# Turning part of the activations by transposing transfers and reordering the end of the attention in a two-layer transformer trunk

## The chip, the cores and the metric

The kernel runs on one core of a Trainium2 chip. The metric is the device time of one execution in microseconds (us), the median of several runs. The engines of the core are named as in the profile: PE is TensorE's matmul pipe and PEld its weight load, DVE is VectorE, ACT is ScalarE, POOL is GpSimd and SP is SyncE, whose queue issues nearly all transfers here.

## The reference

A trunk of two layers works on 256 positions of width 1024. Each layer has a gated feed-forward block, a mixer of three attentions whose outputs are gated and summed, a second feed-forward block and a gated embedding term:

```python
for i in range(DEPTH):
    h = h + 0.5 * swiglu(rms_norm(h, norm_g[i, 0]), ffn1_wi[i], ffn1_wo[i])
    n = rms_norm(h, norm_g[i, 1])
    (aq, ak, av, bq, bkc, bvc, bks, bvs, bkw, bvw, bgate,
     cq, ck, cv, ga, gb, gc) = split_cols(n @ w_in[i], IN_SPLITS)
    ya = diff_attention(...)          # the first attention: aq, ak, av
    yb = nsa_attention(...)           # compressed, selected and windowed keys: b*
    yc = swa_sink_attention(...)      # sliding window with sinks: c*
    merged = (jax.nn.sigmoid(ga) * (ya @ w_branch[i, 0])
              + jax.nn.sigmoid(gb) * (yb @ w_branch[i, 1])
              + jax.nn.sigmoid(gc) * (yc @ w_branch[i, 2]))
    h = h + merged @ w_out[i]
    h = h + 0.5 * swiglu(rms_norm(h, norm_g[i, 2]), ffn2_wi[i], ffn2_wo[i])
    h = h + jax.nn.sigmoid(rms_norm(h, norm_g[i, 3]) @ w_ple_gate[i]) * (p[i] @ w_ple[i])
return rms_norm(h, final_norm)
```

All inputs are float32. The feed-forward width is 2816, each attention has a width of 512, and with 256 positions the selection of blocks in the second attention takes all of them.

## The kernel before

**Number format.** Every large product is done with each operand split into a high and a low part (`split`, line 225: ACT writes the high part, line 228, DVE the rest, line 223), and three matmuls high-high, high-low, low-high (`mul3`, lines 235 to 237). Weights arrive as one stream of tiles of 128x1024 (`load`, line 272): SP issues the transfer (line 278) into one of 4 `raw` buffers, `split` turns it into one of 6 `wh`/`wl` pairs. A product takes its tiles two or three ahead (`AHEAD`).

**Products.** `product` (line 305) runs over the k-tiles of 128 rows for the two position tiles t=0 and t=1. With the usual skew of 8 steps and 8 k-tiles it is first all of t=0, then all of t=1; one step of one tile is three matmuls. After the last k-tile of a position tile it calls `done`, which takes the result out of PSUM.

**Turning.** A matmul wants the left operand with the contraction on the partitions, so activations have to be transposed. `transposes` (line 239) does it on TensorE with the identity as the moving operand, 128x128 at a time, into a `tp` bank of PSUM (3 of them). `Norm.turn` (line 343) turns a half (c=0 or c=1) of a position tile of `h` so, 4 transposes into the bank `nt`, and then ACT and DVE split it with the norm's gain into `nT` (lines 336 and 340). In the attention, `toT` (line 518) turns queries and keys into the bank `qt`: for the first attention from `done_a`, for the second from `done_q` (`qB`) and `done_bk` (`kB`, its second half of columns), for the third from `done_q` (`qC`) and `done_ck` (`kC`, two blocks).

**Turning by transfers.** The feed-forward's gated activations go another way already, `turn_by_dma` (line 436): DVE cuts the float32 values into their two 16-bit halves (`cut`, line 442), SP issues two transposing transfers (`flip`, line 443), and one f-group later `collect` has DVE put the halves together again (`whole`, line 448).

**Attention.** The projections run in the order A0, A1, A2, Ck, Cq, Bk, Bv, Bq. The three attentions are generators in lanes of `Flow` (line 156): each k-step of a product calls `tick`, which advances a lane by a fraction of a step (PACE_A, PACE_B, PACE_C), so that their small pieces lie between the large matmuls. The first attention's branch follows (`branch`, line 954: a gate product, then the branch product `br`), then the compression of the second attention's keys (`compress`, whose rest `compressed` runs in a lane of its own), the branch of the third attention, and last the branch of the second. In this last branch both gate products run first, then `flow.join` finishes the second attention, then the `br` products run for both tiles, column half by column half; `mix` (line 964) adds them to `merged`, turns that on TensorE (`mt`) and splits it to `mT`, which the product `wo` needs.

**The second attention's end.** `attend_b` (line 839) works on units of (group g, position tile t). The last part of a unit multiplies the compressed scores `pcT[t]`; these come from `attend_cmp` (line 803): 12 small matmuls `sc`, a chain of small DVE and ACT operations on `pc` (lines 811 to 822), one transpose `pct` and a copy. It is called inside the unit that first needs them, so that for t=1 it comes near the end.

**Who sets the order.** The program is written in one order, and a scheduler at build time fixes the order of each engine's instructions from it, by readiness and by place in the program; `done` has a higher priority. At run time each engine goes through its list in order and waits at semaphores.

Of the kernel before, what the change touches and what calls it, by code (L numbers as in the profile page):

```python
# [33 lines left out]
PACE_A, PACE_B, PACE_C = 0.75, 0.75, 0.6  # L34
# [121 lines left out]
class Flow:  # L156
# [22 lines left out]
    def join(self, side):  # L179
        while any(s is side for lane in self.lanes.values() for s, _ in lane[0]):  # L180
            for lane in self.lanes.values():
                if lane[0]:
                    self.step(lane)
# [3 lines left out]
def trunk(ctx: ExitStack, tc: tile.TileContext, a: dict, out: bass.AP, index: list):  # L187
    nc = tc.nc
# [20 lines left out]
    def tp_bank(name):  # L209
        return bank("tp", 3, name)  # L210
# [93 lines left out]

    def product(lhs, nk, done, name, w, skew=SKEW):

        def run():
            ps = [None] * NT
            for step in range(nk + skew):
                for t, k in ((0, step), (1, step - skew)):  # L310
# [10 lines left out]
        return run  # L321


    class Norm:
# [18 lines left out]
        def turn(self, t, c):  # L343
            ps = tp_bank("nt")
# [87 lines left out]
    def halves(x):  # L432

        return x.bitcast(U16).rearrange("p (n w) -> p n w", w=2)

    def turn_by_dma(pool, src, m):


        cut = stage("cut").bitcast(U16).rearrange("p (w n) -> p w n", w=2)
        flip = pool.tile([128, 2, 4, 128], U16, tag="flip", bufs=3, name="flip")  # L440
        for w in range(2):
            nc.vector.tensor_copy(cut[:, w, :128 * m], halves(src)[:, :128 * m, w])
            nc.sync.dma_start(flip[:, w, :m], cut[:, w, :128 * m], transpose=True)

        def collect():
            whole = stage("whole")
            for w in range(2):
                tc.keep_in_program_order(nc.vector.tensor_copy(  # L448
                    halves(whole)[:, :128 * m, w], flip[:, w, :m].rearrange("p a b -> p (a b)")))
            return whole[:, :128 * m].rearrange("p (k q) -> p k q", q=128)  # L450
        return collect

    def ffn(i, n, norm, after, aside=None):
# [14 lines left out]
        def gated(f):  # L468
            def done(t, ps):
# [6 lines left out]
                if f % 2 or f == FG - 1:  # L476
                    first, m = f - f % 2, 2 * (f % 2 + 1)
                    pending[t] = 2 * first, m, turn_by_dma(pool, held[t], m)
# [25 lines left out]
    def attention(i, norm, after):  # L504
# [10 lines left out]
        def heads(name):  # L515
            return blk(name).rearrange("p x (k t) q -> p x k (t q)", k=4)

# [137 lines left out]
        def done_bk(t, ps):  # L655
# [3 lines left out]
            for c in range(2):  # L659
# [13 lines left out]
                else:  # L673
                    toT(kB[0], t, slice(0, 4), srcs)
# [15 lines left out]
        def done_q(dst, name):  # L690
            def done(t, ps):
# [4 lines left out]
                toT(dst[0], t, slice(0, 4), [sb[:, 128 * k:128 * k + 128] for k in range(4)])  # L696
# [13 lines left out]
        def compress():  # L710
# [22 lines left out]
            c_sb[0] = pool.tile([128, 512], F32, name="c_sb")  # L733
            nc.vector.tensor_copy(c_sb[0][:64], c_ps[:64])

        def compressed():
# [46 lines left out]
            kc[0] = kt  # L783

# [447 lines left out]
```

## Time and profile before

| | us |
|---|---|
| median of 3 runs | 1357.85 |
| lowest and highest of the 3 | 1355.42, 1359.24 |
| the profiled execution | 1356.52 |
| its span from the first to the last instruction | 1354.7 |
| PE busy in the span | 1331.4 |
| DVE busy | 947.4 |
| ACT busy | 782.2 |

The times of instructions below are from the profiled execution. PE's busy time counts matmuls that overlap: a matmul of 512 columns lasts 390 ns in the record, but the next one starts 227 ns after it. What PE's work costs is therefore read from the distance between starts, not from durations. Layer 2 repeats layer 1 some 668 us later. In layer 1 the mixer runs from about 191 us to 475 us.

### The profile page before, as it was taken

Reading aid. Unit: us, or ns where it says so; the run is one execution under the profiler, and the core shown is the slowest. Engines: PE = TensorE matmul, PEld = TensorE weight load, DVE = VectorE, ACT = ScalarE, POOL = GpSimd, SP = SyncE. Lnnn points to the kernel's source line nnn. Section 1 sums busy time; section 2 is a strip of 40 time slices with the busy share of each in tenths; the row PEclk is TensorE's granted clock in tenths of the full one; section 3 lists DMA queues with packets and bytes.
Section 4 is the critical chain, followed back from the end, with each engine's and each line's share of the span. In section 5 each row is a group of like instructions: output and inputs, shape, how many; then the busy total and the mean of one; then the engine's idle time right before and its main releaser. Section 6 shows DMA issues by size and latency. Waiting matters only on the chain.

```text
span 1354.7 us, 18246 instructions
## 1 busy us (share of the span) xinstructions
PE 1331.4 (98%) x6414; PEld 1096.5 (81%) x6414; DVE 947.4 (70%) x1795; ACT 782.2 (58%) x1382; POOL 18.5 (1%) x36
## 2 busy tenths in 40 slices
PE   9999999999998999999999999999999989999997
PEld 7778888887886788888888888888788868888886
DVE  7677566768887767665767765577697776767565
ACT  7555455668655655544755544566795645545454
POOL 0000000000000000000000000000000000000000
PEclk9999999999999999999999999999999989999999
DMA  8797665444642577775567765645456425887662
GB/s 306 205 275 224 194 226 169 152 166 155 231 154 64 185 201 220 206 221 180 189 198 216 229 202 193 227 151 177 162 186 205 140 65 184 220 222 210 194 204 84
DMA packets 121993, 257.14 MB, mean 190 GB/s; under 512 B 56944, under 2 KB 62500, under 8 KB 121902
## 3 DMA queue, kind: packets, MB, share of 16 engines
q1 hardware_dynamic: 121150, 254.34, 60.5%
q0 software_dynamic: 320, 1.08, 0.3%
q8 instruction: 50, 0.82, 0.2%
q10 hardware_dynamic: 432, 0.56, 0.1%
q14 instruction: 41, 0.34, 0.1%
HBM read 243.33 MB, written 1.08 MB: 180 GB/s over the span
## 4 chain that ended last, share of the span: by engine, by line
PE 92%; DVE 3%; DMA 2%; ACT 2%; issue 1%; SPq 0%; POOLq 0%; POOL 0%; DVEq 0%; ACTq 0%
PE ff L236 11%; PE ff L237 11%; PE ff L235 11%; PE fo L236 6%; PE fo L235 6%; PE fo L237 6%; PE gate L235 3%; PE gate L237 3%; PE gate L236 3%; PE s L537 3%; PE A L236 2%; PE A L235 2%; PE A L237 2%; PE br L236 1%; PE br L235 1%; PE br L237 1%
## 5 line engine op out<-in xcount | busy, mean ns | idle before, releaser
L223 DVE TENSOR_TENSOR wl<-raw,wh 128x1024 fp32r<-128x1024 f32 (+1 forms) x448 | 539.8, 1213 | 176.5 <-ACT wh L228 169.3
L228 ACT ACTIVATE wh<-raw 128x1024 fp32r<-128x1024 f32 (+1 forms) x448 | 467.6, 1050 | 231.6 <-PE fo L237 84.9
L236 PE MATMUL ff<-wl,nT 128*128 128x512 f32 x704 | 273.6, 390 | 2.0 <-DVE wl L223 1.9
L237 PE MATMUL ff<-wh,nT 128*128 128x512 f32 x704 | 273.4, 390 | 0.0
L235 PE MATMUL ff<-wh,nT 128*128 128x512 f32 x704 | 270.8, 391 | 0.0
L236 PEld LDWEIGHTS ff<-wl,nT 128*128 128x128 f32 x704 | 132.2, 188 | 31.3 <-DVE wl L223 4.0
L235 PEld LDWEIGHTS ff<-wh,nT 128*128 128x128 f32 x704 | 132.4, 188 | 29.3 <-ACT wh L228 0.8
L237 PEld LDWEIGHTS ff<-wh,nT 128*128 128x128 f32 x704 | 132.3, 188 | 27.1
L236 PE MATMUL fo<-wl,gT 128*128 128x512 f32 x352 | 134.2, 392 | 0.0
L237 PE MATMUL fo<-wh,gT 128*128 128x512 f32 x352 | 133.7, 389 | 0.0
L235 PE MATMUL fo<-wh,gT 128*128 128x512 f32 x352 | 132.5, 389 | 0.0
L474 ACT ACTIVATE act<-ff,stats 128x256 f32<-128x256 f32 x88 | 41.4, 472 | 86.0 <-PE ff L237 85.8
L475 DVE TENSOR_TENSOR gated<-act,ff 128x256 f32<-128x256 f32 x88 | 36.6, 417 | 65.0 <-ACT act L474 65.0
L235 PEld LDWEIGHTS fo<-wh,gT 128*128 128x128 f32 x352 | 66.1, 188 | 13.9
L235 PE MATMUL gate<-wh,nT 128*128 128x512 f32 x192 | 77.0, 403 | 0.0
L237 PEld LDWEIGHTS fo<-wh,gT 128*128 128x128 f32 x352 | 66.1, 188 | 13.3
L236 PEld LDWEIGHTS fo<-wl,gT 128*128 128x128 f32 x352 | 66.1, 188 | 13.3
L236 PE MATMUL gate<-wl,nT 128*128 128x512 f32 x192 | 75.9, 395 | 0.0
L237 PE MATMUL gate<-wh,nT 128*128 128x512 f32 x192 | 75.8, 395 | 0.0
L228 ACT ACTIVATE gT<-whole 128x512 fp32r<-128x512 f32 (+1 forms) x48 | 28.4, 591 | 62.8 <-DVE whole L448 62.6
L548 ACT ACTIVATE p<-p,st 128x128 f32<-128x128 f32 (+1 forms) x128 | 56.7, 445 | 11.4 <-DVE st L546 11.0
L448 DVE COPY whole<-flip 128x512 uint16<-128x512 uint16 (+1 forms) x96 | 38.2, 434 | 12.8 <-DMA flip<-cut 12.2
(301 smaller groups left out, 2003.2 us busy)
## 6 DMA issues: line engine op xcount, KB each, us to landing
raw<-in_wst SPq DMA_DIRECT2D x438, 512.0 KB, 4.4
band<-table SPq DMA_DIRECT2D x10, 512.0 KB, 4.9
raw<-in_wbv SPq DMA_DIRECT2D x4, 420.0 KB, 3.2
flip<-cut SPq DMA_TRANSPOSE x96, 4.0
xt<-in_xt SPq DMA_DIRECT2D x4, 256.0 KB, 5.2
raw<-in_wst SPq DMA_DIRECT2D x4, 256.0 KB, 3.5
h<-in_x SPq DMA_DIRECT2D x2, 512.0 KB, 7.9
band<-table POOLq DMA_DIRECT2D x2, 512.0 KB, 6.7
```

Source lines behind the costliest of these rows:

```text
L223: nc.vector.tensor_tensor(o, x, y, op=ALU.subtract)
L228: nc.scalar.activation(hi, src, AF.Copy)
L235: nc.tensor.matmul(ps, xh, wh, start=start, stop=False)
L236: nc.tensor.matmul(ps, xh, wl, start=False, stop=False)
L237: nc.tensor.matmul(ps, xl, wh, start=False, stop=stop)
L448: tc.keep_in_program_order(nc.vector.tensor_copy(halves(whole)[:, :128 * m, w], flip[:, w, :m].rearrange("p a b -> p (a b)")))
L474: nc.scalar.activation(act, ps[:, :256], AF.Silu, scale=norm.r(t))
L475: nc.vector.tensor_tensor(held[t][:, 256 * (f % 2):256 * (f % 2) + 256], act, ps[:, 256:], op=ALU.mult)
L537: nc.tensor.matmul(o, q[r, x, qb[m], t * 128:(t + 1) * 128], kk, start=x + y == 0, stop=x == 1)
L548: nc.scalar.activation(p[j], p[j], AF.Exp, bias=st[:, j:j + 1], scale=-1.0, accum_out=st[:, n + j:n + j + 1])
```

## The change

Four things are edited. **First**, `turn_by_dma` is moved out so that all stages can use it, with `flip` in the pool `base` and 2 buffers where it had 3 in the feed-forward's pool, and `Norm.turn` uses it for the half c=0 of each position tile; the half c=1 stays on TensorE. **Second**, `toT_late` does the same for `kB`, `qB`, `qC` and `kC` in the attention. Both put off the second part (`whole` and the split) by 12 product steps, with `later` and `on_time`. **Third**, `attend_cmp` for both position tiles moves to the end of `compressed`, the lane that prepares the compressed keys, and the unit of the second attention only waits until `pcT[t]` is there; PACE_B goes from 0.75 to 0.72. **Fourth**, in the last branch the `br` products are ordered by position tile: t=0 for both column halves as soon as both groups of t=0 are done (`readyB[0] == 2`), then the join, then t=1. To make room, `c_sb` takes a buffer of the tag `th`.

```diff
--- before.py
+++ after.py
@@ -31,7 +31,7 @@
 AHEAD = 2
 RAWS = 4
 WBUFS = 6
-PACE_A, PACE_B, PACE_C = 0.75, 0.75, 0.6
+PACE_A, PACE_B, PACE_C = 0.75, 0.72, 0.6
 
 
 
@@ -176,8 +176,8 @@
                     lane[1] -= 1.0
                     self.step(lane)
 
-    def join(self, side):
-        while any(s is side for lane in self.lanes.values() for s, _ in lane[0]):
+    def join(self, side, ready=lambda: False):
+        while not ready() and any(s is side for lane in self.lanes.values() for s, _ in lane[0]):
             for lane in self.lanes.values():
                 if lane[0]:
                     self.step(lane)
@@ -302,11 +302,24 @@
                 done(t, ps, s)
         return run
 
+    deferred = []
+
+    def later(steps, act):
+
+        deferred.append([steps, act])
+
+    def on_time():
+        for d in deferred:
+            d[0] -= 1
+        while deferred and deferred[0][0] <= 0:
+            deferred.pop(0)[1]()
+
     def product(lhs, nk, done, name, w, skew=SKEW):
 
         def run():
             ps = [None] * NT
             for step in range(nk + skew):
+                on_time()
                 for t, k in ((0, step), (1, step - skew)):
                     if 0 <= k < nk:
                         wh, wl = w(k)
@@ -320,6 +333,27 @@
                         flow.tick()
         return run
 
+    def halves(x):
+
+        return x.bitcast(U16).rearrange("p (n w) -> p n w", w=2)
+
+    def turn_by_dma(src, m):
+
+
+        cut = stage("cut").bitcast(U16).rearrange("p (w n) -> p w n", w=2)
+        flip = base.tile([128, 2, 4, 128], U16, tag="flip", bufs=2, name="flip")
+        for w in range(2):
+            nc.vector.tensor_copy(cut[:, w, :128 * m], halves(src)[:, :128 * m, w])
+            nc.sync.dma_start(flip[:, w, :m], cut[:, w, :128 * m], transpose=True)
+
+        def collect():
+            whole = stage("whole")
+            for w in range(2):
+                tc.keep_in_program_order(nc.vector.tensor_copy(
+                    halves(whole)[:, :128 * m, w], flip[:, w, :m].rearrange("p a b -> p (a b)")))
+            return whole[:, :128 * m].rearrange("p (k q) -> p k q", q=128)
+        return collect
+
 
     class Norm:
         def __init__(self, row):
@@ -341,6 +375,10 @@
                                                T[:, 0, k + m, :].bitcast(F32), op0=ALU.mult, op1=ALU.subtract)
 
         def turn(self, t, c):
+            if c == 0:
+                whole = turn_by_dma(h[:, t, :512], 4)
+                later(12, lambda: self.turned(t, 0, whole().rearrange("p k q -> p (k q)")))
+                return
             ps = tp_bank("nt")
             transposes(ps, [h[:, t, 512 * c + 128 * k:512 * c + 128 * k + 128] for k in range(4)])
             self.turned(t, 4 * c, ps)
@@ -429,27 +467,6 @@
...
-    def turn_by_dma(pool, src, m):
...
-        flip = pool.tile([128, 2, 4, 128], U16, tag="flip", bufs=3, name="flip")
...
@@ -475,7 +492,7 @@
                 nc.vector.tensor_tensor(held[t][:, 256 * (f % 2):256 * (f % 2) + 256], act, ps[:, 256:], op=ALU.mult)
                 if f % 2 or f == FG - 1:
                     first, m = f - f % 2, 2 * (f % 2 + 1)
-                    pending[t] = 2 * first, m, turn_by_dma(pool, held[t], m)
+                    pending[t] = 2 * first, m, turn_by_dma(held[t], m)
             return done
 
         def gathered(t, k):
@@ -514,6 +531,12 @@
 
         def heads(name):
             return blk(name).rearrange("p x (k t) q -> p x k (t q)", k=4)
+
+        def toT_late(dst, t, n, src):
+
+            whole = turn_by_dma(src, n)
+            ts = slice(t * 128, (t + 1) * 128)
+            later(12, lambda: split(dst[:, 0, :n, ts], dst[:, 1, :n, ts], whole()))
 
         def toT(dst, t, blocks, srcs):
 
@@ -671,7 +694,7 @@
                         r = slice(64 * par, 64 * par + 64)
                         nc.vector.tensor_copy(half[0][r, :, t * 64:(t + 1) * 64], v[r, :, :, par])
                 else:
-                    toT(kB[0], t, slice(0, 4), srcs)
+                    toT_late(kB[0], t, 4, sb)
 
         def values(v, ps, scale):
 
@@ -693,7 +716,7 @@
                     dst[0] = heads(name)
                 sb = stage()
                 nc.scalar.activation(sb, ps, AF.Copy, scale=norm.eighth(t))
-                toT(dst[0], t, slice(0, 4), [sb[:, 128 * k:128 * k + 128] for k in range(4)])
+                toT_late(dst[0], t, 4, sb)
             return done
 
         w1 = w2 = None
@@ -730,7 +753,7 @@
                     nc.tensor.matmul(o, both, wh, start=k == 0, stop=False)
                     nc.tensor.matmul(o, both, wl, start=False, stop=k == 15)
                     flow.tick()
-            c_sb[0] = pool.tile([128, 512], F32, name="c_sb")
+            c_sb[0] = pool.tile([128, 512], F32, tag="th", bufs=4, name="c_sb")
             nc.vector.tensor_copy(c_sb[0][:64], c_ps[:64])
 
         def compressed():
@@ -781,6 +804,9 @@
             vc[0] = pool.tile([128, 1, 128], F32R, name="vc")
             values(vc[0], v_ps[:, :64], None)
             kc[0] = kt
+            yield
+            for t in range(NT):
+                yield from attend_cmp(t)
 
         def weighted(y_ps, v, T, start, stop):
 
@@ -798,7 +824,7 @@
             v = tmp.rearrange("p (m q) -> p m q", m=2)
             split(y[:, 0, 2 * g:2 * g + 2, :], y[:, 1, 2 * g:2 * g + 2, :], v)
 
-        yB, pcT = [None] * NT, {}
+        yB, pcT, readyB = [None] * NT, {}, [0] * NT
 
         def attend_cmp(t):
             s_ps = tp_bank("sc")
@@ -883,14 +909,13 @@
                         weighted(y_ps[g, t], vB[0][:, x, k, g], T.rearrange("p x j q -> p x (j q)"), x == 0 and k == 0, False)
                         yield
                 if ss[-1] == 1:
-                    if t not in pcT:
-                        while kc[0] is None:
-                            yield
-                        yield from attend_cmp(t)
+                    while t not in pcT:
+                        yield
                     T = own(t, g)
                     yield
                     weighted(y_ps[g, t], vc[0][:, 0], T.rearrange("p x j q -> p x (j q)"), False, True)
                     gather(yB[t], y_ps[g, t], g)
+                    readyB[t] += 1
                     yield
 
             yield from pipelined([(g, t, ss) for t, sets in ((0, [(0, 1)]), (1, [(0,), (1,)])) for g in range(2) for ss in sets], first, second)
@@ -907,7 +932,7 @@
             dst = sb[:, :256].rearrange("p (x u d) -> p x u d", u=2, d=64)
             nc.scalar.activation(dst[:, :, 0, :], src, AF.Copy, scale=norm.r(t))
             nc.vector.tensor_scalar(dst[:, :, 1, :], src, norm.r(t), None, op0=ALU.mult)
-            toT(kC[0], t, slice(0, 2), [sb[:, 0:128], sb[:, 128:256]])
+            toT_late(kC[0], t, 2, sb)
             values(vC[0][:, t], ps[:, 128:256], norm.r(t))
 
         def attend_c():
@@ -987,9 +1012,22 @@
             if last:
                 for c in range(2):
                     yield gated(c, both[c][0])
+                ws = [streamed(i, f"br{b}{c}", 512) for c in range(2)]
+
+                def tile(t):
+                    for c in range(2):
+                        ps = product_bank(f"br{t}")
+                        for k in range(4):
+                            wh, wl = ws[c](k)
+                            mul3(ps, yT[t][:, 0, k, :], yT[t][:, 1, k, :], wh, wl, k == 0, k == 3)
+                            flow.tick()
+                        with tc.high_priority(offset=150):
+                            both[c][1](t, ps)
+
+                yield lambda: flow.join(sides[side], lambda: readyB[0] == 2)
+                yield lambda: tile(0)
                 yield lambda: flow.join(sides[side])
-                for c in range(2):
-                    yield mixed(c, both[c][1])
+                yield lambda: tile(1)
             else:
                 for c in range(2):
                     yield gated(c, both[c][0])
```

## Rows read from the trace of the kernel before

**Rows 1.** The page's first part: busy time, share, instructions of each engine.
```profile
PE 1331.4 (98%) x6414; PEld 1096.5 (81%) x6414; DVE 947.4 (70%) x1795; ACT 782.2 (58%) x1382; POOL 18.5 (1%) x36
```
**Rows 2.** PE's waits, whole span: who waited for whom; us, times, longest.
```profile
PE pct L243 <- DVE pc L822: 6.2, 2, 3.3
PE pt L243 <- DVE pT L223: 1.9, 2, 0.9
PE mt L243 <- DVE merged L969: 1.3, 2, 0.6
```
**Rows 3.** Stretches: length, busy PE, PEld, DVE, ACT, POOL, clock, DMA share, GB/s.
```profile
220.00:300.00 80.00, 80.00 (x471) 68.02 (x470) 54.95 (x133) 52.20 (x121) 2.78 (x4) 1.00 0.47 156
300.00:360.00 60.00, 60.00 (x344) 48.37 (x343) 54.91 (x147) 52.82 (x127) 0.00 (x0) 1.00 0.59 194
...
409.63:446.66 37.03, 30.92 (x153) 23.62 (x151) 29.97 (x62) 21.98 (x44) 0.00 (x0) 1.00 0.27 85
1077.63:1115.78 38.15, 32.60 (x153) 25.89 (x151) 30.18 (x62) 22.00 (x44) 0.00 (x0) 0.91 0.27 83
1092.80:1099.20 6.40, 5.10 (x22) 4.78 (x23) 4.77 (x10) 3.01 (x7) 0.00 (x0) 0.50 0.00 0
```
**Rows 4.** PE's groups by shape: count, then busy us and mean ns.
```profile
L243 PE MATMUL nt<-ident,h 128*128 128x128 f32 x112 | 16.8, 272 | 0.0
...
L243 PE MATMUL qt<-ident,stage 128*128 128x128 f32 x88 | 15.0, 275 | 0.0
```
**Rows 5.** PE in order of time around one `nt` group: start, us, instruction.
```profile
159.47 0.39 PE L237 MATMUL fo<-wh,gT 128*128 128x512 f32 x1
159.70 0.39 PE L235 MATMUL fo<-wh,gT 128*128 128x512 f32 x1
159.93 0.60 PE L243 MATMUL nt<-ident,h 128*128 128x128 f32 x4
160.29 0.48 PE L236 MATMUL fo<-wl,gT 128*128 128x512 f32 x1
160.60 0.40 PE L237 MATMUL fo<-wh,gT 128*128 128x512 f32 x1
```
**Rows 6.** PE in order of time around the two transposes of `kC`.
```profile
234.85 0.28 PE L236 MATMUL Ck<-wl,nT 128*128 128x256 f32 x1
234.97 0.38 PE L243 MATMUL qt<-ident,stage 128*128 128x128 f32 x2
235.10 0.37 PE L237 MATMUL Ck<-wh,nT 128*128 128x256 f32 x1
```
**Rows 7.** DVE's groups by shape: the copies of turning by transfers.
```profile
L448 DVE COPY whole<-flip 128x512 uint16<-128x512 uint16 x80 | 34.1, 459 | 12.8 <-DMA flip<-cut 12.2
L442 DVE COPY cut<-gated 128x512 uint16<-128x512 uint16 x80 | 30.5, 423 | 1.3
...
L448 DVE COPY whole<-flip 128x256 uint16<-128x256 uint16 x16 | 4.1, 307 | 0.0
L442 DVE COPY cut<-gated 128x256 uint16<-128x256 uint16 x16 | 3.9, 288 | 0.1
```
**Rows 8.** The tile `flip`: issue min/median/max in ns, then time to landing.
```profile
L443 SPq DMA_TRANSPOSE flip<-cut x96: 1179/1210/2118, 31.4 to 1261.6; - x96
...
DMA to landing us min/median/max: 2.3/4.0/7.4
```
**Rows 9.** DVE's and SP's waits, whole span: us in total, times, longest.
```profile
DVE whole L448 <- DMA flip<-cut: 12.2, 15, 1.9
SPq L278 <- DVE wl L223: 524.7, 229, 24.7
```
**Rows 10.** DVE, then PE, at the second attention's end in layer 1.
```profile
419.42 0.28 DVE L811 TENSOR_TENSOR pc<-sc,cbias 128x128 f32<-128x128 f32 x1
...
425.22 0.29 DVE L822 TENSOR_TENSOR pc<-pc,cmask 128x128 f32<-128x128 f32 x1
...
425.57 0.33 PE L243 MATMUL pct<-ident,pc 128*128 128x128 f32 x1 [2.81 <-DVE pc L822]
```

More of the change, by code (lines that the diff above doesn't have):

```diff
@@ L429, in finished @@
             queue.dma_start(out[t * 128:(t + 1) * 128, 512 * k:512 * k + 512], y[k])
-    def halves(x):
-        return x.bitcast(U16).rearrange("p (n w) -> p n w", w=2)
-    def turn_by_dma(pool, src, m):
-        cut = stage("cut").bitcast(U16).rearrange("p (w n) -> p w n", w=2)
-        flip = pool.tile([128, 2, 4, 128], U16, tag="flip", bufs=3, name="flip")
[L441 to L451, printed above, removed]
     def ffn(i, n, norm, after, aside=None):
```

## The prediction

> **What bounds the kernel now.** I read the page's busy times first, then the table of stretches, then PE's waits. PE is busy for 1331.4 of 1354.7 us, DVE for 70% [rows 1]. The stretches show where that share is honest: from 220 to 360 us, where all queries and keys are turned, PE is busy without a break [rows 3], and the waits list names no other place of size than the end of the second attention [rows 2]. Busy PE there means matmuls started back to back: starts of 512 columns stand 0.23 us apart [rows 5]. So outside the attention's end each instruction taken from PE's list shortens the span by its place in the row of starts, as long as weights keep coming. The attention's end is the exception: 37.03 us with 30.92 busy in layer 1, 38.15 with 32.60 in layer 2 [rows 3]. The 6.1 and 5.6 us of idle PE are mostly one wait, the transpose `pct` behind DVE's chain on `pc` (2.8 and 3.3 us) [rows 2, 10]. In layer 2 PE, after that wait, shows a granted clock of 0.50 for 6.4 us [rows 3], the 1.2 GHz level, where layer 1 stays at 2.4 GHz; the same work from gate to `wo` takes 38.15 - 37.03 = 1.1 us longer.
>
> **Transposes taken from PE.** All `nt` transposes are 112 [rows 4], 28 groups of 4; half of them, the 14 groups of c=0, go. Of the 88 `qt` transposes [rows 4] the first attention keeps 32; 12 groups of 4 (`kB`, `qB`, `qC`: two position tiles, two layers) and 4 groups of 2 (`kC`) go. What a group costs is the distance between starts, not 4 x 272 ns: 159.93 to 160.29 is 0.36 us, and the next matmul is followed after 0.31 instead of 0.23, another 0.08 [rows 5]. Two transposes of `kC` take 0.13 [rows 6]. Lower bound: 26 x 0.36 + 4 x 0.13 = 9.9 us; upper, with 0.08 for each group, 12.2 us. The 0.08 is paid where large matmuls follow, as at `nt`; queries and keys often stand beside other small matmuls. I take 14 x 0.44 + 12 x 0.36 + 4 x 0.13 = **11.0 us**, all on the path.
>
> **The end of the second attention.** Moving `attend_cmp` to its own lane takes the chain on `pc` out of the end; there it lasted from 419.42 to 425.51, most of it in DVE's queue behind other pieces [rows 10]. Its 12 `sc` matmuls and one transpose per position tile run earlier, inside products, at the same price. The new `br` order lets 24 matmuls of t=0 (24 x 0.23 = 5.5 us) and the first `wo` matmuls of t=0 run while the last unit of t=1 is finished. At stake are 6.1 + 5.6 us of idle and 1.1 us of clock, 12.8 us; the floor is 0, if the idle only changes its name. What comes last next: weights. The `br` tiles of both halves stay until t=1 is through and take 4 of the 6 `wh`/`wl` pairs, so that only two `wo` tiles are ready; the others are split in the same microseconds in which DVE mixes t=1. Today's waits for `merged` (0.6 us a layer) [rows 2] are of this kind. I leave 1.6 us a layer and take 12.8 - 3.2 = **9.6 us**. The pace of 0.72 only spreads fewer steps; I cost it at nothing, covered by the gate products beside which they lie.
>
> **What it adds.** A moved group of 4 costs DVE two cuts and two copies back, 2 x 0.423 + 2 x 0.459 = 1.76 us, a group of 2 costs 2 x 0.288 + 2 x 0.307 = 1.19 [rows 7]. Over the span that is 26 x 1.76 + 4 x 1.19 = 51 us more, DVE at about 75%: not the bound as a mean. ACT and DVE split as before, from SBUF instead of PSUM; that price I put at nothing, bounded by the 20 to 30 ns by which like groups differ. By stretches it is tighter. From 220 to 360 DVE is busy 54.95 + 54.91 of 140 us, with 5.1 us free in the last 60 [rows 3]. Each layer adds 6 x 1.76 + 2 x 1.19 = 13 us here, which fits into the 30 us free as a sum, but `qB` falls at the edge of the full part. There is no row for DVE falling behind here. Its cost lies between 0 and the two late groups of `qB` with their 3.5 us a layer, 7 us in all; I take **1.5 us**, nearer to 0 because weights are split ahead. Below 0 is excluded: DVE only gains work.
>
> SP issues 60 more transposing transfers at 1.21 us each [rows 8], 73 us of its queue. What is behind one is the weight stream: the issue waits for its `cut`, and the next `raw` transfer with it. SP now waits 525 us for DVE to free a `raw` buffer [rows 9], so it runs ahead; I cost this at nothing, and without that cover it would be one transfer's 2.4 us pair per group, in the tight part only. The DMA share there is 0.47 to 0.59 [rows 3] and leaves room. DVE waits for a landing at the head of `whole`, with the weight splits behind it. From `done` to the second landing: 0.42 + 1.21 + 4.0 = 5.6 us; 12 steps of three matmuls give 12 x 0.68 = 8.2 us. Behind `Ck` and inside `Bv`, with narrow matmuls, they give about 5 us, so two groups a layer may wait for around 1 us. In the feed-forward 96 such copies cost DVE 12.2 us of waits [rows 9]. `flip` with 2 buffers instead of 3 holds at most one turn of each position tile: nothing.
>
> The Trainium skill, page "VectorE: DVE Perf Modes", section "Rules for kernel authors", speaks against the change: a 128x128 transpose belongs on TensorE if PSUM will do as its destination, and the section "The three transpose paths" gives 390 ns there against 1309 ns by transfer (bf16). Charged at 390 ns a piece, the 112 removed transposes would be an estimated 43.7 us, four times what the starts in the rows say; charged at 1309 ns for each half, the transfers would look far dearer, yet they are on no engine that is full.
>
> **Sum.** 1356.5 - 11.0 - 9.6 + 1.5 = **1337 us**, from the profiled execution (span 1354.7, 1.8 around it). It is 1.3 below the median of the runs shown; that is inside the range below and not added.
>
> **Rivals.** (1) *The end of the attention is only moved.* The wait for `pct` goes, but PE then waits for `wo` weights or `mT` as long. For it: the buffers above, and a DMA share of 0.27 there [rows 3], a stream that stands still. Against: 24 ready matmuls where there were 12. Time: 1356.5 - 11.0 + 1.5 = 1347.
>
> (2) *DVE becomes the bound from 220 to 360, and the kernel is slower than before.* The mechanism: `whole` stands at the head of DVE's list until its transfer has landed, and the weight splits wait behind it. Of the 30.1 us that DVE has free there, 13.0 go to copies and 2.4 to a shorter stretch, 14.7 are left. Eight groups a layer with a mean wait w stall PE by 8w - 14.7. The gain of 20.6 us, 10.3 a layer, is eaten at w = 25.0 / 8 = 3.1 us. For it: with the longest landing, 7.4 us [rows 8], a group needs 9.0 us against 8.2, or 4 us more than it has inside `Bv`. Against: the median is 4.0 and the longest wait seen 1.9 [rows 8, 9]; all eight would have to be late. At w = 3.5 the stall is 13.3 a layer: 1356.5 - 20.6 + 26.6 = 1363. The rule of the Trainium skill's page "VectorE: DVE Perf Modes", section "Rules for kernel authors", would show itself here: a slower path whose delay is too short.
>
> (3) *Everything lands.* Upper price of the transposes, no idle left, DVE free: 1356.5 - 12.2 - 12.8 = 1331.5.
>
> (4) *It doesn't do what it says.* The transposes go, but PE's list waits for `nT`, `qB` or weights in their place, and the end of the attention keeps its length: 1355.
>
> **How the numbers follow.** Forecast 1337 (its own range 1332 to 1343): 0.55. Rival 1: 0.17. Rival 2: 0.09. Rival 3: 0.12. Rival 4: 0.07. The measurement tells about 0.3% (4 us) from no change. Faster: 0.55 + 0.17 + 0.12 = 0.84; same: rival 4, 0.07; slower: 0.09. The range reaches from below rival 3, by the 1.1 us between the profiled execution and the fastest run and some rounding, to above rival 1: 1329 to 1350. It leaves out rivals 2 and 4 and little else.
>
> **What would show it.** `nt` falls to 56 and `qt` to 32, `flip` rises from 96 to 156 issues; the wait of `pct` is gone from PE's waits, and the stretch from the last gates to `wo` loses 4 to 6 us a layer with the clock at 1.00 in both. Where t=0's half c=0 ends in `fo`, the starts stay 0.23 us apart instead of 0.36 across the `nt` group. Right on DVE: its busy time is near 998 us, its wait for `flip` stays under 30 us, and PE stays unbroken from 220 to 360. Wrong: PE waits for `wl` in 300 to 360, or for `whole` through `nT` or `qB`, or a new wait of 3 us or more between the `br` and `wo` products.

## The result: slower by 0.5%

The changed kernel takes 1364.76 us (median of 4 runs, 1363.40 to 1366.04), the kernel before 1357.55 beside it: ratio 1.0054, interval 1.0036 to 1.0072. The forecast was 1337 us, with a range of 1329 to 1350. The profiled execution took 1364.21 us, its span 1362.4 against 1354.7.

The page's first part of the changed kernel answers to [rows 1]. PE has 112 instructions less, as forecast, and DVE 38 us more work, where 51 were forecast; but PE's busy time fell by 5.3 us only, and 7.7 us were added to the span.

```profile
PE 1326.1 (97%) x6302; PEld 1089.0 (80%) x6302; DVE 985.5 (72%) x1915; ACT 780.8 (57%) x1382; POOL 19.7 (1%) x36
```

PE's waits in the changed kernel (us in total, times, longest) answer to [rows 2]. `pct` is gone. New is a wait of 5.5 us in each layer, `ct` behind `stage<-Bk` on DVE, and there are smaller ones at the end of the attention and ahead of the feed-forwards. `ct` is the transpose of `Bk`'s result for the compression; `stage<-Bk` is the instruction that takes this result out of PSUM, its evacuation.

```profile
PE ct L243 <- DVE stage L687: 11.0, 2, 5.5
PE mt L243 <- DVE merged L994: 3.4, 2, 1.7
PE br L235 <- ACT th L987: 2.6, 2, 1.5
...
PE yb L813 <- ACT mT L231: 1.6, 2, 0.8
...
PE nt L243 <- DVE h L415: 1.4, 2, 0.7
PE wo L235 <- ACT mT L231: 1.4, 2, 0.7
...
PE ff L235 <- ACT nT L370: 1.0, 3, 0.4
```

The next two fences cut layer 1 by starts of PE's products: from the first matmul of `Ck` to the first of the compression, and from there to the first of the second feed-forward (columns as in [rows 3]). Before:

```profile
227.25:332.57 105.32, 105.32 (x610) 87.37 (x610) 78.23 (x196) 76.16 (x184) 2.78 (x4) 1.00 0.49 164
332.57:467.30 134.73, 128.62 (x667) 104.76 (x666) 107.44 (x254) 83.95 (x174) 0.55 (x1) 1.00 0.47 154
```

After, with two shorter stretches around `ct`:

```profile
226.26:341.62 115.36, 109.53 (x603) 90.07 (x603) 92.10 (x256) 79.71 (x204) 2.77 (x4) 0.96 0.57 167
262.50:268.40 5.90, 0.41 (x3) 0.17 (x2) 5.69 (x13) 2.92 (x5) 0.00 (x0) 0.77 0.83 255
268.40:276.00 7.60, 7.59 (x39) 7.15 (x40) 5.93 (x14) 2.27 (x7) 0.00 (x0) 0.51 0.37 107
341.62:471.65 130.03, 124.53 (x640) 101.43 (x638) 103.48 (x225) 77.18 (x148) 0.00 (x0) 0.99 0.50 159
```

The first stretch is 10.0 us longer (9.7 in layer 2), the second 4.7 us shorter (6.3). PE stands idle for 5.5 us at `ct`, and in the next 7.6 us the granted clock is 0.51, the 1.2 GHz level, with PE busy throughout: half of that, 3.7 us, is lost once more. So this place costs 9.2 us a layer, some 18 us in all. The first stretch also holds 21 matmuls more than before less its 28 transposes (610 - 28 = 582, not 603): pieces of the attentions slide ahead of the compression, which lengthens it and shortens the next one.

DVE in order of time, changed kernel, before `ct` starts at 268.40 (start, us, instruction, idle time ahead of it):

```profile
258.18 0.74 DVE L223 TENSOR_TENSOR wl<-raw,wh 128x560 fp32r<-128x560 f32 x1 [4.87 <-ACT wh L228]
...
264.80 0.87 DVE L638 SCALAR_TENSOR_TENSOR p<-p,st 128x256 f32<-128x256 f32 x2
265.59 1.21 DVE L223 TENSOR_TENSOR wl<-raw,wh 128x1024 fp32r<-128x1024 f32 x1
266.72 0.47 DVE L232 SCALAR_TENSOR_TENSOR yA<-yt,sg,yA 128x256 fp32r<-128x256 f32 x1
267.12 0.77 DVE L352 COPY whole<-flip 128x512 uint16<-128x512 uint16 x2
267.79 0.47 DVE L687 TENSOR_SCALAR stage<-Bk,stats 128x256 f32<-128x256 f32 x1
```

The tile `flip` from 243 to 262 us (issues: min/median/max in ns, first and last start; then landing):

```profile
L347 SPq DMA_TRANSPOSE flip<-cut x4: 1194/1238/2159, 245.0 to 252.1; - x4
...
DMA to landing us min/median/max: 2.4/3.3/4.2
```

`stage<-Bk` stands directly behind the two copies `whole` of `qC`. They don't wait for their transfer: the last of these issues starts at 252.1 and the longest lands after 4.2 us, by 256.3, while `whole` runs at 267.12. It has its place in DVE's list behind softmax pieces of the first attention, three weight splits and `yA`. In the kernel before, `stage<-Bk` ran at 258.60, 9.2 us earlier:

```profile
258.60 0.48 DVE L664 TENSOR_SCALAR stage<-Bk,stats 128x256 f32<-128x256 f32 x1 [0.97 <-ACT stage L663]
```

The late evacuation holds more than `ct`. In the attention the products take turns in two PSUM banks (`mm`), so `Bv` can start only when the first bank of `Bk` has been taken out: in the changed kernel the instruction that holds PE back for `Bv` is through at 269.7, when the second `stage<-Bk` of this bank ends. PE's list has changed with it. In the kernel before, 24 matmuls of `Bv` and 12 of `s` run ahead of `ct`, which starts at about the same time as in the changed kernel and waits for nothing (PE in order of time, before, then after):

```profile
264.31 0.29 PE L235 MATMUL Bv<-wh,nT 128*128 128x280 f32 x1
...
268.48 0.60 PE L243 MATMUL ct<-ident,stage 128*128 128x128 f32 x4
```

```profile
268.40 1.09 PE L243 MATMUL ct<-ident,stage 128*128 128x128 f32 x4 [5.49 <-DVE stage L687]
...
271.32 0.60 PE L235 MATMUL Bv<-wh,nT 128*128 128x280 f32 x1
```

### The profile page after: what moved, and what is told of

It reads as the page before. It is cut to its first block, busy times and chain, and to the rows that moved or that the text cites. A ratio compares the mean times of both kernels' runs of the same rounds, so it can differ in the third digit from the quotient of the medians.

```text
span 1362.4 us, 18213 instructions
## 1 busy us (share of the span) xinstructions
PE 1326.1 (97%) x6302; PEld 1089.0 (80%) x6302; DVE 985.5 (72%) x1915; ACT 780.8 (57%) x1382; POOL 19.7 (1%) x36
## 4 chain that ended last, share of the span: by engine, by line
PE 87%; DVE 5%; ACT 3%; DMA 2%; issue 2%; SPq 0%; POOL 0%; POOLq 0%; DVEq 0%; ACTq 0%
PE ff L236 11%; PE ff L237 11%; PE ff L235 11%; PE fo L237 6%; PE fo L236 6%; PE fo L235 6%; PE gate L235 3%; PE gate L236 3%; PE gate L237 3%; DVE wl L223 2%; PE s L560 2%; PE A L237 2%; PE A L236 2%; PE A L235 2%; PE br L235 1%
## 5 line engine op out<-in xcount | busy, mean ns | idle before, releaser
L352 DVE COPY whole<-flip 128x512 uint16<-128x512 uint16 (+1 forms) x156 | 61.4, 434 | 21.7 <-DMA flip<-cut 20.9
L237 PEld LDWEIGHTS fo<-wh,gT 128*128 128x128 f32 x352 | 66.1, 188 | 13.5
```

The lines of the kernel that those rows point to most:

```text
L237: nc.tensor.matmul(ps, xl, wh, start=False, stop=stop)
L352: tc.keep_in_program_order(nc.vector.tensor_copy(halves(whole)[:, :128 * m, w], flip[:, w, :m].rearrange("p a b -> p (a b)")))
```

## The experiments

Theory A at the start: the loss is this one wait, it comes from the queries and keys alone, and the end of the attention has only moved its idle time. Theory B: DVE's added work costs a little everywhere.

### The three parts alone

Each run is the full change with the other parts undone. For the end alone, norms, queries and keys go back to PE (`kB` and `kC` like `qB`):

```
-            if c == 0:
-                whole = turn_by_dma(h[:, t, :512], 4)
-                later(12, lambda: self.turned(t, 0, whole().rearrange("p k q -> p (k q)")))
-                return
...
-                toT_late(dst[0], t, 4, sb)
+                toT(dst[0], t, slice(0, 4), [sb[:, 128 * k:128 * k + 128] for k in range(4)])
```

> The kernel before with only the new end of the second attention (compressed attention in its own lane, new order of the br tiles, pace 0.72, c_sb in a th buffer); no transpose is moved. Theory A (one new wait: the changed kernel's loss sits at ct behind stage<-Bk, 5.5 us idle and about 3.8 us of clock in each layer, 18.6 us in all, and comes from the queries and keys alone; the end of the attention has only moved its idle): 1357 us, within 2 us of before, with no wait for pct and other waits in its place. Theory B (the DVE work that transfers add, 38 us, costs a little everywhere; the end gives what was forecast, 9.6 us): 1348 us.

Measured: 1346.18 us, ratio 0.9912 (0.9895 to 0.9928), 12.0 less than the kernel before beside it. For the end B's number holds and A is wrong. PE's waits of this run:

```profile
PE yb L809 <- DVE yt L819: 1.9, 4, 0.8
...
PE wo L235 <- ACT mT L231: 1.6, 2, 0.8
...
PE mt L243 <- DVE merged L990: 1.4, 2, 0.7
```

Its two stretches of layer 1:

```profile
227.84:333.13 105.29, 105.29 (x611) 87.37 (x611) 78.19 (x196) 76.22 (x184) 2.78 (x4) 1.00 0.49 163
333.13:463.02 129.89, 126.67 (x668) 104.11 (x666) 106.72 (x250) 83.83 (x169) 0.00 (x0) 1.00 0.47 160
```

The idle time behind the compression goes from 6.1 to 3.2 us in this layer, no wait in the two attentions is over 0.8 us, and the clock stays at 1.00 in both layers.

For the norms alone, and for queries and keys alone, the end goes back:

```
-            yield
-            for t in range(NT):
-                yield from attend_cmp(t)
...
-                yield lambda: flow.join(sides[side], lambda: readyB[0] == 2)
-                yield lambda: tile(0)
                 yield lambda: flow.join(sides[side])
-                yield lambda: tile(1)
+                for c in range(2):
+                    yield mixed(c, both[c][1])
```

> The kernel before with only the c=0 halves of the norms turned by transfer (14 groups; flip in the base pool with 2 buffers, c_sb in a th buffer because the attention's pool is 1.5 KB too small otherwise). Theory A: the price of a group from the starts holds, 14 x 0.44 = 6.2 us less, 1351 us. Theory B: the added DVE work (14 x 1.76 = 25 us) and DVE's waits for landings eat it, 1355 to 1360 us.

Measured: 1356.56 us, ratio 0.9985 (0.9973 to 0.9997), 1.6 less, as B had it. PE's busy time fell from 1331.4 to 1325.2 us, as much as the sum, but that is no measure of the transposes: the end alone, with all 6414 instructions, took 5.5 us off it. The span of the profiled execution, 2.9 us faster than the run's median, fell by 2.8 us only; the wait that grew most is at the end of the attention, where [rows 2] have 0.6 us (PE's waits of this run):

```profile
PE mt L243 <- DVE merged L993: 3.4, 2, 2.7
```

> The kernel before with only the queries and keys of the second and third attention turned by transfer (12 groups of 4 and 4 of 2). Theory A: 4.8 us of transposes less, 18.6 us for the wait at ct and its clock more, 1371 us, with the wait ct behind stage<-Bk in PE's list at 5.5 us in each layer. Theory B: 26 us more of DVE, spread, 1358 to 1362 us, and the wait at ct smaller than in the full change.

Measured: 1368.49 us, ratio 1.0073 (1.0058 to 1.0088), 10.3 more, near A. The wait at `ct` is the one of the full change, and `pct` still waits as in [rows 2] (PE's waits of this run):

```profile
PE ct L243 <- DVE stage L683: 11.0, 2, 5.5
PE pct L243 <- DVE pc L841: 6.3, 2, 3.2
```

So the loss is the queries' and keys'. But the parts sum to -12.0 - 1.6 + 10.3 = -3.3, and together they give +7.2.

### What makes `ct` wait: load, buffers or order

Two theories more: C, too few `stage` buffers; D, the order in which the scheduled program hands DVE its work. Three runs each change one of these in the full change, a fourth moves `whole` by four steps. The fifth buffer needs room, so its run also puts the compression's `gl` and `hid` into buffers of other tiles (not shown here).

```
-        return base.tile([128, 512], F32, tag="stage", bufs=4, name=name)
+        return base.tile([128, 512], F32, tag="stage", bufs=5, name=name)
```

> The full change with 5 instead of 4 stage buffers (gl and hid of the compression moved into buffers of other small tiles to make the room). Theory C (too few stage buffers: cut and whole hold them until their transfers land): the wait at ct goes, 20 us less than the full change, 1345 us. Theory D (order: the copies whole are pinned to the order of the program on DVE, behind pieces of the first attention, and stage<-Bk, which takes a buffer of the same tag after whole, follows them; no number of buffers helps): within 3 us of 1365 us, the wait at ct stays 5.5 us in each layer.

Measured: 1357.91 us, ratio 1.0000 (0.9990 to 1.0009). `ct` waits as long as with four (PE's waits of this run):

```profile
PE ct L243 <- DVE stage L687: 11.1, 2, 5.5
PE mt L243 <- DVE merged L994: 1.4, 2, 0.7
```

C falls as the cause of this wait. The 6.9 us that the run is faster by were in neither expectation. In its profiled execution, which is 4.5 us faster than its median, they lie mostly behind the compression (125.4 us in layer 1 instead of 130.0), where `mt` waits 0.7 instead of 1.7 us. Whether the buffer or the move of `gl` and `hid` gives them, no run separates.

```
-                sb = stage()
+                sb = pool.tile([128, 512], F32, tag="th", bufs=4, name="sb")
                 src = ps[:, 256 * c:256 * c + 256]...
```

> The full change, but the two staging tiles that Bk's results are copied to are taken from the th buffers (free at that time) instead of the stage buffers; whole stays pinned. Theory D (order): stage<-Bk no longer follows whole on DVE; ct comes as in the kernel before; the stretch from Ck to the compression, 10.0 and 9.7 us longer in the full change, becomes about 2 us shorter than before in each layer: 1340 to 1345 us. Theory C (number of buffers): the same. Theory B (DVE's added load is what delays ct): at least 1358 us, and another wait on DVE in the same stretch.

Measured: 1359.83 us, ratio 1.0011 (1.0000 to 1.0022). The wait at `ct` is gone, as D says, for DVE's list now has `stage<-Bk` ahead of `whole`. But the time is B's, since others wait in the same stretch, first of all `Bv` for the rest of `Bk`'s evacuation (`sb` here), so a second wait stood behind that of `ct` (PE's waits of this run):

```profile
PE Bv L235 <- DVE sb L687: 4.9, 2, 2.4
PE ya L235 <- ACT pT L228: 4.1, 2, 2.1
```

```
-                tc.keep_in_program_order(nc.vector.tensor_copy(...))
+                nc.vector.tensor_copy(...)
```

> The full change with the copies whole not pinned to the order of the program. Theory D (order): whole runs when its transfer has landed, some 10 us earlier for qC, stage<-Bk follows it in time, the wait at ct goes: 1340 to 1347 us. Theory C (number of buffers): 4 buffers as before, little change, at least 1358 us. Theory B (load): at least 1358 us.

Measured: 1354.41 us, ratio 0.9975 (0.9962 to 0.9988), 10.4 below the full change. DVE runs `whole` of `qC` 16 us earlier and `stage<-Bk` at 256.72, and the stretch from `Ck` to the compression is 105.49 us long, as before the change. DVE in order of time in this run:

```profile
250.77 0.80 DVE L352 COPY whole<-flip 128x512 uint16<-128x512 uint16 x2
...
256.72 0.48 DVE L687 TENSOR_SCALAR stage<-Bk,stats 128x256 f32<-128x256 f32 x1 [2.60 <-ACT stage L686]
```

The two stretches of layer 1 in this run:

```profile
226.32:331.81 105.49, 104.35 (x584) 85.32 (x583) 87.96 (x228) 76.01 (x185) 4.12 (x4) 1.00 0.65 183
331.81:467.25 135.44, 129.09 (x659) 105.22 (x657) 106.57 (x252) 81.07 (x166) 0.00 (x0) 0.99 0.48 153
```

DVE does the same work in this run as in the full change (983.7 and 985.5 us), so load doesn't explain the wait; D does. D's time was 7 us too low: the stretch behind is 135.4 us long, where the end alone has 129.9, and no run shows why.

```
-            later(12, lambda: split(dst[:, 0, :n, ts], dst[:, 1, :n, ts], whole()))
+            later(16, lambda: split(dst[:, 0, :n, ts], dst[:, 1, :n, ts], whole()))
```

> The full change, with the copies whole of queries and keys asked for 16 instead of 12 matmul steps after their transfer (whole of qC then stands four steps of Bk later in the program, right ahead of Bk's own result; pin, buffers and load are the same). Theory D (order): what whole is pinned behind changes, so the wait at ct changes strongly, to less than 2 us: 1345 to 1352 us. Theory B (load) and theory C (buffers, held a little longer): 1363 to 1368 us, as in the full change.

Measured: 1351.24 us, ratio 0.9946 (0.9931 to 0.9961), within D's numbers and 13.5 below the full change, by a move of four steps. By the starts of the products, 9.5 of the 15.2 us between the two profiled spans are won from `Ck` to the compression. No wait at `ct` is left; three smaller ones stand around it (PE's waits of this run):

```profile
PE ya L237 <- DVE pT L223: 3.1, 2, 1.6
...
PE Bv L235 <- ACT sig L710: 1.9, 2, 0.9
PE yt L243 <- DVE yn L662: 1.7, 2, 0.8
```

What follows: the order of DVE's list makes the wait. Taking the pin, the place in the program or the shared buffer tag out of it ends the wait each time; a fifth buffer under the same tag doesn't. By which rule the scheduler gives the pinned `whole` its place isn't shown: with 16 steps it stands ahead of the same `yA`.

### Why the parts don't add up

E: queries and keys regain some of their delay in the idle time that the old end leaves. F: end and norms both need `stage` buffers. G: norms and queries disturb each other.

> The full change without the queries and keys (their transposes stay on PE): norms' c=0 halves by transfer, and the new end of the second attention. Alone the end gave 12.0 us less, the norms 1.6 less, queries and keys 10.3 more, 3.3 us less as a sum, where all together gave 7.2 more. Theory E (the end and the queries and keys don't add up: alone, the delay of queries and keys is partly regained in the idle time that the end of before leaves, and with the new end it is not): 1342 to 1346 us, as the sum of end and norms. Theory F (the end and the norms don't add up, as both need stage buffers at the end of the attention): 1350 to 1354 us, with mt waiting for merged 1.7 us and a clock under 0.95 around wo, as in the full change.

Measured: 1348.72 us, ratio 0.9939 (0.9924 to 0.9954), between the two. On top of the end the norms cost 2.5 us instead of giving 1.6; the intervals of the two runs still overlap a little. The diff is that of the end alone without its first hunk. `mt` waits for `merged` as in the full change (PE's waits of this run):

```profile
PE mt L243 <- DVE merged L994: 3.4, 2, 1.7
```

Where `wo` starts in layer 1 the clock falls (a stretch of 8 us in this run, and its second half); in layer 2 the same wait of 1.7 us leaves it at 1.00:

```profile
444.00:452.00 8.00, 5.60 (x20) 3.94 (x19) 5.84 (x10) 2.97 (x5) 0.00 (x0) 0.79 0.53 148
...
448.00:452.00 4.00, 4.00 (x12) 3.02 (x13) 1.84 (x3) 0.00 (x0) 0.00 (x0) 0.59 0.71 221
```

The end alone in the same place keeps it at 1.00 and runs 34 matmuls in 8 us instead of 20:

```profile
441.00:449.00 8.00, 6.53 (x34) 5.10 (x33) 6.17 (x9) 3.51 (x6) 0.00 (x0) 1.00 0.42 142
```

The next three runs add the fifth buffer, as above, to the run of norms and end, to the unpinned one and to the one with 16 steps.

> As the run of norms and end, with 5 stage buffers (gl and hid of the compression in buffers of other small tiles). Theory E: the same as with 4 buffers, within 2 us. Theory F: 6 to 10 us less than with 4 buffers, 1341 to 1346 us; mt waits for merged 0.7 us instead of 1.7 in each layer.

Measured: 1348.78 us, ratio 0.9937 (0.9922 to 0.9951), the same as with four, and `mt` still waits 1.7 us. F falls.

> The full change with both edits that each took a part of the loss away: whole not pinned (took the stretch from Ck to the compression back to before's length, 10 us a layer) and 5 stage buffers (took 4 to 5 us a layer from the stretch behind it). If the two losses are two mechanisms (order on DVE; stage buffers at the end): 1354.4 less 8 or 9, 1345 us. If the fifth buffer only gave back the delay that ct's wait had made: 1354 us, no gain over the unpinned run.

Measured: 1356.51 us, ratio 0.9990 (0.9980 to 1.0001): nothing gained over 1354.41.

> The full change with whole of queries and keys asked for 16 instead of 12 steps later and with 5 stage buffers. Two mechanisms: the stretch behind the compression gets shorter by the 4 us a layer that it did with 12 steps, 1343 to 1347 us. One mechanism: 1351 us, as with 4 buffers.

Measured: 1349.03 us, ratio 0.9947 (0.9928 to 0.9966), against 1351.24 with four; the intervals overlap. The fifth buffer clearly helps only where `ct` waits. Why it helps there isn't settled.

The last two leave out the norms (the first hunk of the first diff); the second of them also has 16 steps.

> The new end and the queries and keys by transfer, without the norms. Alone they gave -12.0 and +10.3 us, a sum of -1.7 (1356.5 us). Queries and keys cost 16.1 us on top of end and norms, where alone they cost 10.3. Theory E (the new end has no idle left in which the delay of queries and keys is regained): 1346.2 + 16 = 1362 us. Theory G (it is the norms that the queries and keys disturb, by shared flip and stage buffers): 1356 to 1358 us.

Measured: 1360.42 us, ratio 1.0021 (1.0012 to 1.0030). Queries and keys cost 14.2 us on top of the end, nearer to E's 16 than to G's 10.3. By the starts of the products, the stretch behind the compression is 2.8 and 5.2 us shorter than before in the run of queries and keys alone, but only 2.1 and 2.9 us shorter than the end's own in this one. That is 3 us in the profiled executions, where the medians differ by 3.9.

> As the run of end and queries and keys, with whole asked for 16 instead of 12 steps later. With the norms this step took the full change from 1364.8 to 1351.2 us. If the order around whole is all that makes queries and keys dear, they now cost no more than 3 us on top of the end: 1346 to 1349 us. If transferring them has a price of its own (waits that move but stay): 1351 us or more.

Measured: 1352.68 us, ratio 0.9958 (0.9942 to 0.9975), 6.5 above the end alone. So transferring queries and keys has a price of its own. The profiled execution is the fastest of four (1350.5 to 1355.5 us, at mean clocks of 0.999 down to 0.991) and 3.9 us above that of the end alone; what the others lose with the clock no trace shows. In the profiled one PE's busy time is 6.0 us below the end alone (1319.9 against 1325.9), and no stretch of the attentions has a lower clock, but the waits are back under other names. PE's waits of this run:

```profile
PE ya L237 <- DVE pT L223: 3.0, 2, 1.5
PE gate L235 <- ACT stage L714: 2.3, 2, 1.2
PE kc L235 <- ACT hid L228: 2.0, 2, 1.2
...
PE Bv L235 <- ACT sig L706: 1.9, 2, 0.9
```

### The end, edit by edit

The end alone with the order of the `br` tiles as before:

```
...
-                yield lambda: flow.join(sides[side], lambda: readyB[0] == 2)
-                yield lambda: tile(0)
                 yield lambda: flow.join(sides[side])
-                yield lambda: tile(1)
+                for c in range(2):
+                    yield mixed(c, both[c][1])
```

> The new end alone without its new order of the br tiles: only the compressed attention moves to its own lane (and c_sb, and the pace). The prediction put the wait for pct (6.2 us in the page of before) to the lane, the rest of 12.8 us to the order. If so: 1358 - 6 = 1352 us, the wait for pct gone, the other idle time of the end still there. If the lane alone moves the idle time to another wait: 1356 us or more. If the order adds nothing: 1346 us.

Measured: 1348.17 us, ratio 0.9924 (0.9907 to 0.9941), 9.6 less than before. The lane gives most of the 12.0 us; the order of the `br` tiles takes `mt`'s longest wait from 2.7 to 0.7 us and adds some 2 us, though the intervals of the two runs overlap. The lane's expectation of 6 us was too small: it counted the wait for `pct` alone. PE's waits of this run:

```profile
PE mt L243 <- DVE merged L990: 3.3, 2, 2.7
```

And with the pace as before:

```
-PACE_A, PACE_B, PACE_C = 0.75, 0.72, 0.6
+PACE_A, PACE_B, PACE_C = 0.75, 0.75, 0.6
```

> The new end alone with the second attention's pace left at 0.75. The prediction costed the pace at nothing: 1346 us, within 2 us. If the pace is what fits the longer work of the other lane into the gate products: 1350 us or more.

Measured: 1345.89 us, ratio 0.9909 (0.9894 to 0.9924). The pace costs and gives nothing that shows. This run and the end alone beat the kernel before by 0.9%, and the changed one by more.

## Why the prediction was wrong

**Transposes: the size was right, "all on the path" was not.** Starts show the size. Each stretch from the first matmul of `fo`, the output product of a feed-forward, to the next product held 12 `nt` transposes and holds 4, and goes from 61.3 to 60.3 us, in the run of the norms alone as in the full change. That is 1.0 us for two groups, where 0.88 were forecast, or 0.12 us of PE's list for a 128x128 transpose. The Trainium skill, page "VectorE: DVE Perf Modes", section "The three transpose paths", has 390 ns for one in bf16; here one in float32 lasts 0.27 us [rows 4] and takes less than half of that from the list. For queries and keys no run shows the size by itself: the 6.0 us of busy time fit the 4.8 of the sum with the 0.08 us after a group that it left out for them, but busy time moves as much without a transpose less (the full change and the run with 16 steps, of the same instructions, differ by 6.2). The upper price in the sum should be 12.3 us, not 12.2; nothing hangs on it.

What failed here is the step from PE's list to the span. [Rows 3] had PE without a break from 220 to 360, and I took that for a reserve. It only said that each operand came in time in the order of that program. At each hand-over to a feed-forward the changed kernel gives back about what it won. PE in order of time, changed kernel (in the kernel before, the `nt` group comes after three `ff` matmuls and none of them waits):

```profile
684.01 0.60 PE L243 MATMUL nt<-ident,h 128*128 128x128 f32 x4
...
685.07 0.50 PE L235 MATMUL ff<-wh,nT 128*128 128x512 f32 x1 [0.23 <-ACT nT L370]
...
686.13 0.50 PE L235 MATMUL ff<-wh,nT 128*128 128x512 f32 x1 [0.33 <-ACT nT L370]
```

The other half of the norm, still on PE, stands some eight matmuls later in PE's list, and `nT` comes late for the fifth step. In the two feed-forwards behind `wo`, PE also waits 0.7 us for `h` ahead of its second `nt` group, a wait that the kernel before doesn't have. From `ff` to `fo` three of the four feed-forwards are 1.1 to 1.2 us longer than before, where two groups had given 1.0.

**The end of the attention: right, and too small.** 9.6 us were forecast, 12.0 measured, with the clock at 1.00 in both layers, as the stake of 12.8 had it. Most of it is the lane's: by itself it gives 9.6. Rival 1 (the idle time only moves) is refuted for the end by itself. In the full change, `mt` waits 1.7 us and the clock falls around `wo`, which comes with the norms' transfers: with the end, queries and keys alone, `mt` waits 0.7.

**What it adds: the step that failed.** I put it at 1.5 us, as load on DVE and as waits for landings. Both were small indeed: DVE waits 20.9 us for `flip` over the whole span, under the 30 forecast (DVE's waits, changed kernel):

```profile
DVE whole L352 <- DMA flip<-cut: 20.9, 20, 2.2
```

I priced each new copy by its duration and its transfer, and not by its place. `whole` carries a pin in the diff, and its tile shares a tag with `stage<-Bk`; the prediction gives neither a price. In each layer they put the evacuation that `ct` and `Bv` need 9.2 us later than before, and the wait and the clock behind it cost 9.2 us a layer too, some 18 us in all against the 1.5 forecast. By the starts of the products the whole loss adds up: 19.8 us more from `Ck` to the compression in both layers, 11.0 less behind it, 4.8 less in the four `fo` stretches and the embedding term, and 3.5 more in the three feed-forwards make 7.5 of the 7.7 us.

**Rival 2** named the stretch and nearly the time, 1363, by another mechanism: it had DVE full and `whole` waiting for its transfer. DVE had in fact been idle for 4.87 us from 253.3, waiting for ACT's `wh`, and the transfers were in by 256.3. Its deciding point, a mean wait of 3.1 us a group for a landing, is nowhere near: all waits for `flip` grew by 8.7 us, and even if they were all those of the 16 groups of queries and keys, that is 0.5 us each.

**Costed at nothing.** The pace: rightly. SP's queue: no run tests it by itself, and PE's wait for weights at `ff` is 1.8 us in the changed kernel and 1.9 before. `flip` with 2 buffers: not tried. `stage` buffers weren't considered; the run with five is 6.9 us faster while `ct` waits, and not clearly faster where it doesn't.

The Trainium skill, the same page, section "Rules for kernel authors", keeps a 128x128 transpose on TensorE if PSUM will do. For queries and keys the runs agree: with the new end in place, they cost 6.5 to 14.2 us by transfer, though by order and waits rather than by the transfer's duration. For the norms they leave it open: 1.6 us gained alone, 2.5 lost with the new end.

## What to carry over

An engine that is busy without a break in a trace shows that its operands arrive in time in that order; it is no promise for another order. Price a step that is moved to another engine by what stands ahead of it and behind it in that engine's list, pins and shared buffer tags included, and look at the scheduled list before the sum. Ask also what else a late evacuation holds: here the bank of the next product. Split a change with several parts and time each: here one part of three held nearly all of the gain.

## What the runs showed of the hardware

A wait of 5.5 us on PE cost 9.2: the granted clock stayed at 0.51 for 7.6 us after it, with PE busy. In the run of norms and end, the wait of 1.7 us for `mt` in layer 1 was followed by 4 us at 0.59; the same wait in layer 2, and those of 0.7 us with the end alone, were followed by no lower clock.
